# Weight-block differences of the FFNs' first pairs: formed by accumulating transfers in the place of VectorE's subtractions

## The chip, the cores and the metric

The kernel runs on one core of a Trainium2 chip. The metric is the device time of one execution in microseconds (us), as the median of several runs. Engines are named as the profile names them: PE is TensorE, DVE VectorE, ACT ScalarE, POOL GpSimd, SP SyncE.

## The reference

One layer of an encoder, 1024 tokens, model width 1024, FFN width 2816, float32. Only the two FFNs matter here:

```python
def swiglu(x, w_gate, w_up, w_down):
    return (jax.nn.silu(x @ w_gate) * (x @ w_up)) @ w_down
...
h = h + 0.5 * swiglu(rms_norm(h, ffn1_norm[i]), ffn1_w_gate[i], ffn1_w_up[i], ffn1_w_down[i])
...
h = h + (g_attn * y_attn + g_ssm * y_ssm) @ w_out[i]
h = h + 0.5 * swiglu(rms_norm(h, ffn2_norm[i]), ffn2_w_gate[i], ffn2_w_up[i], ffn2_w_down[i])
```

Between them lie attention and a state-space mixer, whose parameters are prepared by small operations while the first FFN runs.

## The kernel before

**Split products.** Every float32 operand is split into a high and a low part, so that one product is three matmuls of 128 x 512: high by high (L180), high by low (L181), low by high (L182). `split` (L148) makes the parts of a tile: ACT casts the high part (L149), DVE subtracts it from the source to get the low one (L150). Parts of weights are named wh and wl, parts of the x side xh and xl.

**Seven products.** The FFN matmuls are done in blocks of two by two by a scheme with seven products in the place of eight. The width 2816 is cut into 22 blocks of 128, which form 11 pairs, p = 0 to 10. Pair 0 is done plainly. In each other pair there are 14 items ("A", p, i, g): product i = 0 to 6, g = gate or up. An item is 12 matmuls into PSUM banks named gx, gy, gz, ux, uy, uz. In pair 1 the x operands (s1 to s4 and plain blocks) are still being made by DVE (L494 to L503) and split; later pairs use them again. After the A items come the B items of the down projection.

**Weight operands.** For each p and g there are four raw blocks b11, b12, b21, b22, tiles of `hbuf`, and `b_operand` (L421) makes the operand of product i out of them, in place, and splits it:

```python
if i in (2, 3, 6):
    V.tensor_tensor(b11, (b12, b22, None, None, b21)[i - 2], b11, ALU.subtract)
elif i == 5:
    V.tensor_tensor(b12, b22, b12, ALU.subtract)
hi, lo = tw("wh", [P, HT]), tw("wl", [P, HT])
mark["ins"] = split(hi, lo, (b21, b11, b11, b11, b22, b12, b11)[i]).ins
```

So the operands are: b21 for i = 0, b11 for 1, b12 - b11 for 2, b22 less that for 3, b22 for 4, b22 - b12 for 5, and b21 less the block that product 3 left in b11 for 6. Below, "(1,5,gate)" is the item p = 1, i = 5, g = gate. The down projection calls `b_operand` too, for its own tiles (wblk).

**Loads.** `load_two` (L460, its DMA at L465) brings b11 and b12, or b21 and b22, of one p and g with one transfer of 512 KB on SP's queue, as soon as the tiles of pair p - 2 are free. In pairs 1 and 2 one k is loaded ahead of the other.

**Order.** `run` (L697) prepares operands `la` items ahead: 4 in the first FFN, 8 in the second. PE's order is the program's throughout. DVE and ACT follow the program's order up to item (2,0,gate) of the first FFN; after that a scheduler orders them when the program is built. POOL and SP are ordered by it all through. Each engine carries out its instructions in order, so one that waits holds back all behind it. Evacuations (`evac_a`): for i = 0, 2, 3 ACT copies the bank (L576); for others DVE adds it to an earlier one (L580), then ACT applies silu for the gate (L584) or DVE multiplies gate and up (L586); `combine` (L531 to L539) makes four sums of hidden blocks.

**Beside it.** In the first FFN a generator prepares the mixer: POOL copies columns of `pw` into g_pe and g_pg (L867, L870), then multiplies them into gm, tv, em, tg (L922 to L924); PE transposes the results (L947, L958).

Of the kernel before, what the change touches and what calls it, by code (L numbers as in the profile page):

```python
# [11 lines left out]
AF = mybir.ActivationFunctionType  # L12
ALU = mybir.AluOpType
# [5 lines left out]
HT = 512  # L19
# [19 lines left out]
def encoder_block(ctx, tc, I, out):  # L39
    nc = tc.nc  # L40
    V, A, G, T = nc.vector, nc.scalar, nc.gpsimd, nc.tensor
# [26 lines left out]
    def at(kind, shape, dt, name):  # L68
        pool, tag, bufs = cur[kind]
        return pool.tile(list(shape), dt, tag=tag, bufs=bufs, name=name)  # L70
# [4 lines left out]
    def tw(name, shape=(P, 1024), dt=F32R):  # L75
        return at("w", shape, dt, name)
# [60 lines left out]
    def force():  # L137
        side["wait"] = 0
        tick()
# [8 lines left out]
    def split(hi, lo, src, eng=V):  # L148
        A.copy(hi, src)  # L149
        return eng.tensor_tensor(lo, src, hi.bitcast(F32), ALU.subtract)  # L150
# [267 lines left out]
                    self.put(name, self.h[j0 + k][1])  # L418
                    yield 1

    def b_operand(blk, i):  # L421

        b11, b12, b21, b22 = blk
        if i in (2, 3, 6):
            V.tensor_tensor(b11, (b12, b22, None, None, b21)[i - 2], b11, ALU.subtract)  # L425
        elif i == 5:
            V.tensor_tensor(b12, b22, b12, ALU.subtract)
        hi, lo = tw("wh", [P, HT]), tw("wl", [P, HT])
        mark["ins"] = split(hi, lo, (b21, b11, b11, b11, b22, b12, b11)[i]).ins
        return hi, lo  # L430

    NP2 = NF // 2
    C4 = ("11", "12", "22", "21")

    class Ffn:
# [175 lines left out]
        def prep(self, item):  # L611
            if item[0] == "C":
                _, c, g = item
                if c in ("11", "12") and not self.seven.plain:
                    for n in ((0, 2) if c == "11" else (1, 3)):
                        if ("C", g, n) in self.made:
                            continue
                        hi, lo = self.two[n, g]
                        mark["ins"] = split(hi, lo, self.blocks[0][g][n]).ins
                        self.made["C", g, n] = hi, lo  # L620
                return
            if item[0] == "A":
                _, p, i, g = item
                while self.stage < (1 if i < 2 else 2, 3)[p > 1]:
                    force()
                self.made[item] = b_operand(self.blocks[p][g], i)
                return
            _, i, j = item
            raw = self.kept.pop((i, j))
            hi, lo = at("tmp", [P, HT], F32R, "ah"), at("tmp", [P, HT], F32R, "al")  # L630
            split(hi, lo, raw)
            self.made[item] = (hi, lo), b_operand(self.blocks["d", j], i)
# [799 lines left out]
    for hp in range(4):  # L1432
# [3 lines left out]
        n = 2 if hp < 3 else 6  # L1436
# [294 lines left out]
```

## Time and profile before

| | us |
|---|---|
| median of 3 runs | 2145.44 (2139.88 to 2147.64) |
| the profiled execution | 2143.34 |
| its span in the trace | 2141.6 |
| PE busy | 2099.0 (98%) |
| DVE busy | 1423.1 (66%) |
| ACT busy | 986.9 (46%) |
| POOL busy | 395.0 (18%) |

The span runs from the first to the last record of the trace. Rows of a timeline carry the start of an instruction, its duration, and in brackets the engine's idle time before it with what ended the wait. Windows give the busy time of each engine in a stretch of the span and the clock granted to PE there, as a share of full speed. Mean durations overlap by the engines' pipelines: DVE's 128 x 512 subtractions show 0.68 us each, and follow each other every 0.60 to 0.61.

### The profile page before, as it was taken

The page shows a single profiled execution, that of the slowest core. Times are in us where ns is not written, and L with a number is a line of the kernel's source. Part 1 is how long each engine was busy: PE and PEld are TensorE (multiplying, and loading weights), DVE is VectorE, ACT ScalarE, POOL GpSimd, SP SyncE. Part 2 cuts the span into 40 slices and gives each one's busy share as a digit, 9 for nine tenths or more (in the row PEclk, how much of TensorE's full clock was granted, in tenths as well). Part 3 has the DMA queues.
Part 4 walks back from the last instruction along what each step waited for, and adds up shares of the span by engine and source line. Part 5 has one row for each costly group of instructions (what it writes and reads, how often), then busy time and mean ns, then how long its engine had stood idle before and what let it go on. Part 6 is the DMA issues. An engine that isn't in the chain of part 4 may idle for free.

```text
span 2141.6 us, 28452 instructions
## 1 busy us (share of the span) xinstructions
PE 2099.0 (98%) x9708; PEld 1718.3 (80%) x9708; DVE 1423.1 (66%) x2462; ACT 986.9 (46%) x1831; POOL 395.0 (18%) x680
## 2 busy tenths in 40 slices
PE   8999999999999999999999999999999999999997
PEld 3688888878888888888887788788888888888886
DVE  7886776666967334767744666896566565785845
ACT  6433333334445334666874432553333334445643
POOL 0047555540000008888000000000000000000000
PEclk9999999999999999999999999999999999999998
DMA  3524343466533452223576732242423338533302
GB/s 131 160 84 158 121 139 119 143 213 227 183 115 117 141 177 81 70 75 100 147 212 213 238 100 64 95 155 85 134 83 110 107 99 288 169 106 92 118 21 79
DMA packets 201105, 282.06 MB, mean 132 GB/s; under 512 B 42624, under 2 KB 85760, under 8 KB 200960
## 3 DMA queue, kind: packets, MB, share of 16 engines
q1 hardware_dynamic: 186112, 259.27, 38.1%
q10 hardware_dynamic: 14848, 20.98, 2.8%
q8 instruction: 76, 1.25, 0.3%
q14 instruction: 69, 0.57, 0.1%
HBM read 197.86 MB, written 82.31 MB: 131 GB/s over the span
## 4 chain that ended last, share of the span: by engine, by line
PE 87%; DVE 4%; DMA 4%; ACT 3%; issue 1%; SPq 1%; DVEq 0%; ACTq 0%
PE dx L180 4%; PE dx L181 4%; PE dx L182 4%; PE gx L180 3%; PE gx L182 3%; PE gx L181 3%; PE ux L180 3%; PE ux L182 3%; PE ux L181 3%; PE dy L180 2%; PE dy L182 2%; PE dy L181 2%; PE uy L180 2%; PE gy L180 2%; PE gy L182 2%; PE uy L182 2%
## 5 line engine op out<-in xcount | busy, mean ns | idle before, releaser
L149 ACT CAST wh<-hbuf 128x512 fp32r<-128x512 f32 x280 | 173.0, 622 | 396.0 <-PE gx L181 87.3
L150 DVE TENSOR_TENSOR wl<-hbuf,wh 128x512 fp32r<-128x512 f32 x280 | 208.9, 748 | 129.7 <-ACT wh L149 129.4
L149 ACT CAST wh<-wblk 128x512 fp32r<-128x512 f32 x162 | 100.4, 622 | 162.7 <-PE dx L181 67.5
L150 DVE TENSOR_TENSOR al<-araw,ah 128x512 fp32r<-128x512 f32 x154 | 106.2, 693 | 57.3 <-PE dx L181 19.7
L150 DVE TENSOR_TENSOR wl<-wblk,wh 128x512 fp32r<-128x512 f32 x162 | 112.1, 694 | 43.1 <-ACT wh L149 39.0
L180 PE MATMUL dx<-ah,wh 128*128 128x512 f32 x352 | 138.1, 392 | 0.5 <-DVE hbuf L693 0.5
L182 PE MATMUL dx<-ah,wl 128*128 128x512 f32 x352 | 137.0, 389 | 0.0
L181 PE MATMUL dx<-al,wh 128*128 128x512 f32 x352 | 137.0, 389 | 0.0
L1095 POOL TENSOR_TENSOR sc<-X,rho 128x128 f32<-128x128 f32 x128 | 72.4, 566 | 341.8 <-ACT X L1078 331.8
L180 PE MATMUL gx<-xh,wh 128*128 128x512 f32 x320 | 125.8, 393 | 5.7 <-DVE c L580 5.7
L182 PE MATMUL gx<-xh,wl 128*128 128x512 f32 x320 | 125.3, 391 | 0.0
L181 PE MATMUL gx<-xl,wh 128*128 128x512 f32 x320 | 125.0, 391 | 0.0
L180 PE MATMUL ux<-xh,wh 128*128 128x512 f32 x320 | 124.8, 390 | 0.0
L182 PE MATMUL ux<-xh,wl 128*128 128x512 f32 x320 | 124.5, 389 | 0.0
L181 PE MATMUL ux<-xl,wh 128*128 128x512 f32 x320 | 124.5, 389 | 0.0
L149 ACT CAST ah<-araw 128x512 fp32r<-128x512 f32 x154 | 94.9, 619 | 51.8 <-PE dx L181 12.6
L180 PE MATMUL gt<-xh,wh 128*128 128x512 f32 x256 | 103.2, 403 | 0.0
L182 PE MATMUL gt<-xh,wl 128*128 128x512 f32 x256 | 100.2, 392 | 0.0
L181 PE MATMUL gt<-xl,wh 128*128 128x512 f32 x256 | 100.1, 391 | 0.0
L425 DVE TENSOR_TENSOR hbuf<-hbuf 128x512 f32<-128x512 f32 x120 | 89.1, 743 | 2.5 <-DMA hbuf<-in_wu 0.5
L180 PEld LDWEIGHTS dx<-ah,wh 128*128 128x128 f32 x352 | 66.1, 188 | 15.9 <-DVE hbuf L693 1.7
L181 PEld LDWEIGHTS dx<-al,wh 128*128 128x128 f32 x352 | 66.1, 188 | 13.9 <-issue 0.5
(375 smaller groups left out, 5761.4 us busy)
## 6 DMA issues: line engine op xcount, KB each, us to landing
araw<-a_d SPq DMA_DIRECT2D x154, 256.0 KB
a_d<-c SPq DMA_DIRECT2D x148, 256.0 KB
wblk<-in_wd SPq DMA_DIRECT2D x88, 256.0 KB
hbuf<-in_wg SPq DMA_DIRECT2D x40, 512.0 KB
hbuf<-in_wu SPq DMA_DIRECT2D x40, 512.0 KB
wst<-in_win SPq DMA_DIRECT2D x26, 512.0 KB
hbuf<-in_xT SPq DMA_DIRECT2D x32, 256.0 KB
h_d<-hbuf ACTq DMA_DIRECT2D x32, 256.0 KB
```

Source lines behind the costliest of these rows:

```text
L149: A.copy(hi, src)
L150: return eng.tensor_tensor(lo, src, hi.bitcast(F32), ALU.subtract)
L180: T.matmul(o, lhsT=wh, rhs=xh, start=first, stop=False, skip_group_check=more)
L181: T.matmul(o, lhsT=wh, rhs=xl, start=False, stop=False, skip_group_check=more)
L182: T.matmul(o, lhsT=wl, rhs=xh, start=False, stop=last, skip_group_check=more)
L425: V.tensor_tensor(b11, (b12, b22, None, None, b21)[i - 2], b11, ALU.subtract)
L1095: G.tensor_tensor(sc, both, rho4, ALU.mult)
```

## The change

In pairs 1 to 3 of the first FFN and pairs 1 and 2 of the second, `b_operand` gets `src`, the four blocks of the weights in HBM. It subtracts nothing then. After the split of product 1, 2 or 3 it calls `taken_from`: ACT negates a raw block in place, and POOL issues a transfer of 256 KB that adds a block of the weights from HBM to it. After product 1, b11 becomes b12 - b11; after product 2, b11 becomes b22 less that and b12 becomes b22 - b12; after product 3, b11 becomes the operand of product 6. Each block's subtraction is thereby replaced by one negation and one transfer, four for each p and g, and the transfer is issued one or more products ahead of the operand's use. Lines below move by 10 or 13.

```diff
--- before.py
+++ after.py
@@ -418,15 +418,25 @@
                     self.put(name, self.h[j0 + k][1])
                     yield 1
 
-    def b_operand(blk, i):
+    def taken_from(blk, i, src):
+
+        A.activation(blk[i], blk[i], AF.Copy, scale=-1.0)
+        G.dma_start(blk[i], src, accum_op=ALU.add)
+
+    def b_operand(blk, i, src=None):
+
 
         b11, b12, b21, b22 = blk
-        if i in (2, 3, 6):
+        if src is None and i in (2, 3, 6):
             V.tensor_tensor(b11, (b12, b22, None, None, b21)[i - 2], b11, ALU.subtract)
-        elif i == 5:
+        elif src is None and i == 5:
             V.tensor_tensor(b12, b22, b12, ALU.subtract)
         hi, lo = tw("wh", [P, HT]), tw("wl", [P, HT])
         mark["ins"] = split(hi, lo, (b21, b11, b11, b11, b22, b12, b11)[i]).ins
+        if src is not None and i in (1, 2, 3):
+            taken_from(blk, 0, src[(1, 3, 2)[i - 1]])
+            if i == 2:
+                taken_from(blk, 1, src[3])
         return hi, lo
 
     NP2 = NF // 2
@@ -623,7 +633,10 @@
                 _, p, i, g = item
                 while self.stage < (1 if i < 2 else 2, 3)[p > 1]:
                     force()
-                self.made[item] = b_operand(self.blocks[p][g], i)
+                src = None
+                if p < (4 if self.seven.plain else 3):
+                    src = [self.w[g][p + (n % 2) * NP2][:, (n // 2) * HT:(n // 2 + 1) * HT] for n in range(4)]
+                self.made[item] = b_operand(self.blocks[p][g], i, src)
                 return
             _, i, j = item
             raw = self.kept.pop((i, j))
```

**Where the orders differ.** First DVE in pair 1 of the first FFN, at the operands of (1,2,gate) and (1,2,up). The names c_434 and c_438 are the same tile; s_315 and the like are x operands. Before:

```order
L558 TENSOR_TENSOR c_434<-g_397,rs_113 128x512 [waits PE_49]
L425 TENSOR_TENSOR hbuf<-hbuf 128x512 [waits DMAHW1_49]
L150 TENSOR_TENSOR wl<-hbuf,wh 128x512 [waits Activation_49]
L500 TENSOR_TENSOR s_315<-s_315,hbuf 128x512
L500 TENSOR_TENSOR s_318<-s_318,hbuf 128x512
L500 TENSOR_TENSOR s_321<-s_321,hbuf 128x512
L150 TENSOR_TENSOR xl<-s_315,xh 128x512 [waits Activation_49]
L500 TENSOR_TENSOR s_331<-s_331,hbuf 128x512
L150 TENSOR_TENSOR xl<-s_318,xh 128x512 [waits Activation_49]
L425 TENSOR_TENSOR hbuf<-hbuf 128x512 [waits DMAHW2_49]
```

and with the change:

```order
L568 TENSOR_TENSOR c_438<-g_397,rs_113 128x512 [waits PE_49]
L150 TENSOR_TENSOR wl<-hbuf,wh 128x512 [waits DMASW0_49,Activation_49]
L510 TENSOR_TENSOR s_315<-s_315,hbuf 128x512
L510 TENSOR_TENSOR s_318<-s_318,hbuf 128x512
L510 TENSOR_TENSOR s_321<-s_321,hbuf 128x512
L150 TENSOR_TENSOR xl<-s_315,xh 128x512 [waits Activation_49]
L510 TENSOR_TENSOR s_331<-s_331,hbuf 128x512
L150 TENSOR_TENSOR xl<-s_318,xh 128x512 [waits Activation_49]
```

L425 is gone, and wl waits for a transfer of POOL's queue (DMASW) beside ACT's cast.

Second ACT, from the cast of (1,4,up) to the first cast of pair 2, with the change (L586 and L594 are L576 and L584 of before). The two L423 wait for a transfer of SP's queue (DMAHW1, DMAHW2) and are the negations of b12 of pair 3; the first stands ahead of the cast of (1,6,gate), the second behind that of (2,0,gate).

```order
L149 CAST wh<-hbuf 128x512
L586 COPY c_610<-uy 128x512 [waits PE_49]
L149 CAST wh<-hbuf 128x512 [waits DMASW3_49]
L586 COPY c_641<-gx 128x512 [waits PE_49]
L149 CAST wh<-hbuf 128x512 [waits DMASW5_49]
L586 COPY c_659<-ux 128x512 [waits PE_49]
L423 ACTIVATE hbuf<-hbuf 128x512 [waits DMAHW1_49,DVE_49]
L149 CAST wh<-hbuf 128x512 [waits DMASW7_49]
L594 ACTIVATE c_641<-c_641 128x512 [waits DVE_49]
L149 CAST wh<-hbuf 128x512 [waits DMASW0_49]
L149 CAST wh<-hbuf 128x512 [waits DMAHW6_49,PE_49]
L423 ACTIVATE hbuf<-hbuf 128x512 [waits DMAHW2_49,Activation_49]
```

The casts of (1,5,gate) to (1,6,up), which waited for DVE before, now wait for transfers of POOL's queue (DMASW), and the negations of b12 for loads.

Third POOL, at the end of the generator's copies, in pair 3 of the first FFN. Before:

```order
L870 COPY g_pg<-pw 128x16
L867 COPY g_pe<-pw 128x16
L922 TENSOR_TENSOR gm<-g_pg,bb 128x512 [waits Pool_49]
L923 TENSOR_TENSOR tv<-g_pg,bb 128x512 [waits DMAHW1_49,Pool_49]
L922 TENSOR_TENSOR em<-g_pe,bc 128x576 [waits DVE_49,Pool_49]
L923 TENSOR_TENSOR tg<-g_pe,bc 128x576
L924 TENSOR_TENSOR gm<-gm,tv 128x512 [waits Pool_49]
L924 TENSOR_TENSOR em<-em,tg 128x576 [waits Pool_49]
```

and with the change, where L880 and L883 are the copies and L935 to L937 the products:

```order
L883 COPY g_pg<-pw 128x16
L880 COPY g_pe<-pw 128x16
L424 DMA hbuf<-in_wg 128x512 [waits DMAHW3_49,DMASW2_49,Activation_49]
L424 DMA hbuf<-in_wu 128x512 [waits DMAHW4_49,DMASW3_49,Activation_49]
L935 TENSOR_TENSOR gm<-g_pg,bb 128x512 [waits Pool_49]
L936 TENSOR_TENSOR tv<-g_pg,bb 128x512 [waits DMAHW1_49,Pool_49]
L935 TENSOR_TENSOR em<-g_pe,bc 128x576 [waits DVE_49,Pool_49]
L936 TENSOR_TENSOR tg<-g_pe,bc 128x576
L937 TENSOR_TENSOR gm<-gm,tv 128x512 [waits Pool_49]
L424 DMA hbuf<-in_wg 128x512 [waits DMASW4_49,Activation_49]
L424 DMA hbuf<-in_wu 128x512 [waits DMASW5_49,Activation_49]
L937 TENSOR_TENSOR em<-em,tg 128x576 [waits Pool_49]
```

The transfers of pair 3's products 2 stand behind all copies, those of product 3 behind five of the generator's products.

## Rows read from the trace of the kernel before

**Rows 1.** The page: busy time by engine, and one group of the costliest ones.

```profile
PE 2099.0 (98%) x9708; PEld 1718.3 (80%) x9708; DVE 1423.1 (66%) x2462; ACT 986.9 (46%) x1831; POOL 395.0 (18%) x680
...
L149 ACT CAST wh<-hbuf 128x512 fp32r<-128x512 f32 x280 | 173.0, 622 | 396.0 <-PE gx L181 87.3
```

**Rows 2.** PE's waits: line, releaser, us in total, times, longest us.

```profile
PE gx L180 <- DVE c L580: 5.7, 2, 4.5
```

**Rows 3.** PE's timeline: start us, us, operation [idle time before it, releaser].

```profile
64.69 0.80 PE L180 MATMUL gz<-xh,wh 128*128 128x512 f32 x1
...
102.46 0.47 PE L180 MATMUL gx<-xh,wh 128*128 128x512 f32 x1 [4.53 <-DVE c L580]
...
103.42 0.63 PE L180 MATMUL gx<-xh,wh 128*128 128x512 f32 x1
...
106.89 0.39 PE L180 MATMUL ux<-xh,wh 128*128 128x512 f32 x1
...
158.62 0.39 PE L180 MATMUL gy<-xh,wh 128*128 128x512 f32 x1
...
164.06 0.39 PE L180 MATMUL gx<-xh,wh 128*128 128x512 f32 x1
```

**Rows 4.** Windows: stretch, length, busy us by engine, PEclk, DMA share, GB/s.

```profile
94.00:98.00 4.00, 3.94 (x18) 2.84 (x16) 2.83 (x5) 1.71 (x4) 0.97 (x3) 1.00 0.84 239
...
104.00:106.00 2.00, 2.00 (x7) 1.52 (x6) 1.97 (x4) 0.01 (x1) 0.00 (x0) 0.50 0.20 77
...
110.00:150.00 40.00, 40.00 (x178) 33.12 (x177) 36.74 (x125) 15.50 (x28) 15.45 (x57) 1.00 0.30 100
...
1400.00:1450.00 50.00, 50.00 (x222) 41.39 (x221) 44.73 (x74) 24.53 (x45) 0.00 (x0) 1.00 0.49 163
1450.00:1500.00 50.00, 50.00 (x223) 41.38 (x222) 32.72 (x52) 17.95 (x31) 0.00 (x0) 1.00 0.27 90
```

**Rows 5.** DVE's groups by line, 64.5 to 102 us: busy, mean ns | idle before.

```profile
L150 DVE TENSOR_TENSOR wl<-hbuf,wh 128x512 fp32r<-128x512 f32 x11 | 7.6, 690 | 5.7 <-ACT wh L149 5.7
L425 DVE TENSOR_TENSOR hbuf<-hbuf 128x512 f32<-128x512 f32 x6 | 4.1, 684 | 0.0
...
L427 DVE TENSOR_TENSOR hbuf<-hbuf 128x512 f32<-128x512 f32 x2 | 1.4, 682 | 0.0
```

**Rows 6.** DVE's timeline in pair 1 of the first FFN.

```profile
61.70 2.50 DVE L150 TENSOR_TENSOR wl<-hbuf,wh 128x512 fp32r<-128x512 f32 x4 [1.21 <-ACT wh L149]
...
67.41 0.69 DVE L150 TENSOR_TENSOR wl<-hbuf,wh 128x512 fp32r<-128x512 f32 x1 [0.69 <-ACT wh L149]
...
88.28 0.69 DVE L150 TENSOR_TENSOR wl<-hbuf,wh 128x512 fp32r<-128x512 f32 x1 [0.74 <-ACT wh L149]
...
101.63 0.68 DVE L580 TENSOR_TENSOR c<-gx,c 128x512 f32<-128x512 f32 x1
```

**Rows 7.** SP's timeline (loads issued), then ACT's (waits for loads).

```profile
1.19 0.41 SPq L981 DMA_DIRECT2D hbuf<-in_xT  x1
...
89.00 0.54 SPq L465 DMA_DIRECT2D hbuf<-in_wg  x1
...
1399.19 0.56 SPq L465 DMA_DIRECT2D hbuf<-in_wg  x1
...
3.85 1.28 ACT L345 ACT_TABLE_LOAD   x1 [3.85 <-DMA hbuf<-in_xT]
...
1403.14 0.62 ACT L149 CAST wh<-hbuf 128x512 fp32r<-128x512 f32 x1 [0.92 <-DMA hbuf<-in_wg]
```

**Rows 8.** POOL's timeline in pairs 2 and 3 of the first FFN.

```profile
147.61 0.21 POOL L870 COPY g_pg<-pw 128x16 f32<-128x16 f32 x1
...
152.32 0.67 POOL L870 COPY g_pg<-pw 128x16 f32<-128x16 f32 x1
...
154.57 1.05 POOL L922 TENSOR_TENSOR gm<-g_pg,bb 128x512 f32<-128x512 f32 x1
...
159.77 1.75 POOL L924 TENSOR_TENSOR gm<-gm,tv 128x512 f32<-128x512 f32 x1
```

## The prediction

> **What bounds the kernel now.** I read the busy shares first: PE is busy 2099.0 us, 98% of the span [rows 1]. So whatever DVE is relieved of pays only where PE waits for DVE. The second view, PE's waits, lists one wait in the stages that the change touches, gx at L180 behind DVE's L580: 5.7 us in two stalls, the longest 4.5 [rows 2]. PE's timeline places that one in pair 1 of the first FFN, before item (1,6,gate): PE is idle for 4.53 us up to 102.46 [rows 3]. The rest of the windows say that there is no second place: PE is busy 3.94 of the last 4 us before it, 40.00 of 40 from 110 to 150, and 50.00 of 50 in both windows of the second FFN's pairs 1 and 2 [rows 4].
>
> The stall costs more than its idle time. After it the granted clock stands at 0.50 (the 1.2 GHz level) from 104 to 106 [rows 4], and one matmul shows 0.63 us where it shows 0.39 before [rows 3]. The item that follows the gap runs from 102.46 to 106.89, 4.43 us; the 14 items of a pair at full clock follow each other at 2.72 us (the two from 158.62 to 164.06 take 5.44) [rows 3]. So the stall costs 4.53 + 1.71 = 6.2 us, and that is all that the change can win from PE: 0.29% of the run. A measurement of this kernel tells about 0.5%, 10.7 us, from no change.
>
> **Why DVE is late there.** Between 64.5 and 102 us DVE runs L425 six times and L427 twice, each 0.68 us long, and before eleven wl it stands idle 5.7 us in all, behind ACT's cast wh [rows 5]. The chain of one operand is visible in [rows 6]: subtract, wait for ACT's cast, wl. DVE's own order then puts L580 on gx behind all of it, at 101.63 [rows 6], and PE waits for its end.
>
> **The change, part by part.** *Removed:* 40 subtractions, 24 in pairs 1 to 3 of the first FFN and 16 in pairs 1 and 2 of the second. In pair 1 the eight free 8 x 0.60 us (DVE's pitch: 2.50 us for four, less 0.69 for the last, by three [rows 6]) plus most of the 5.7 us of waiting, some 10 us. In the other four stages PE never waited, so those 32 are worth nothing.
>
> *Added on ACT:* 40 negations. No row shows one; a cast of the same tile takes 622 ns on ACT [rows 1], and I take that. *Added on POOL and the DMA engines:* 40 accumulating transfers of 256 KB. The trace has none. Call D the time from the negation's end to the landed sum. From below: a plain 256 KB load, issued at 1.19, had landed by 3.85, 2.66 us [rows 7]. From above: a 512 KB load issued at 1399.19 releases ACT's cast at 1403.14, 3.95 us [rows 7]; two of these in series (the sum must read and write its destination too) and the longest POOL row of 1.75 us for the issue [rows 8] make 9.6. I take 4.5: the sum touches twice the bytes of a 256 KB load, as the 512 KB load does (3.95), and an issue costs 0.54 on SP [rows 7].
>
> POOL is not a neutral place to issue from. Its small copies take 0.21 us alone and 0.67 beside DVE's two-input operations [rows 8]; an issue slowed in that ratio would add about 1 us to D. The Trainium skill has a rule that speaks against this (SBUF — State Buffer, SBUF: two separate sides): descriptors of transfers issued from GpSimd are written by GpSimd and starve while VectorE runs an operation in a 2-port mode. It also says that a two-input operation contends only with GpSimd's reads; no run here shows an issue beside either. By the Trainium skill, DMA: Bandwidth & Descriptors (Anatomy of one DMA), the transfer itself would be 2.0 us plus bytes at 436 GB/s, an estimate of 2.6 us, and the sum would be that of the first rival below.
>
> **The walk with D = 4.5.** *Pair 1.* The third of the four wl that start at 61.70 ends near 63.6 [rows 6]; negation to 64.2; landed 68.7; cast and wl of (1,2,gate) end at 70.1, where the wl of before ended at 68.10. ACT now has two negations, 1.2 us, ahead of the two xh casts, so (1,3,gate) ends its wl near 78.2 and (1,3,up) near 81.3, 1.7 us later than before. PE wants them at 64.69 + 6 x 2.72 = 81.0 and 83.7, so nothing stalls; the x operand s4, delayed by the same 1.7, still arrives. From there on DVE gains: wl (1,5,gate), which ended at 88.97 [rows 6], loses a subtraction and a cast wait (1.34) and ends near 89.3; the rest of the way to L580 on gx loses three subtractions and three waits, 3.9 us, so gx could start near 98.1. But a new wait sits in ACT's queue: the negation of pair 3's b12 stands ahead of the cast of (1,6,gate), and it needs a load that SP issues only when wl (1,5,gate) has freed its buffers (89.00 before [rows 7]). At 3.95 to 5 us landing, ACT resumes at 93.3 to 94.3, and wl (1,6,gate) and gx slip by up to 1.5. PE, which wants gx at 97.9, then waits 1 to 2.5 us instead of 4.53, and gets a shorter dip of clock: loss 3 us in the place of 6.2. **Term: -3.2.**
>
> *Pair 2.* Operands are prepared four items beyond the one at work, up to 13.6 us ahead; two steps of D + 1.9 (cast, wl, negation) against a cadence of 5.44 lose 2 x 1.0 us of it. Term 0.
>
> *Pair 3.* Its sums for products 2 stand in POOL's queue behind the generator's copies, those for product 3 behind gm, tv, em, tg, gm as well. The copies ended before at 154.57 [rows 8], but many of them were slowed by DVE, which now stands still itself, blocked in its order at wl (3,2,gate) from about 145, but for four combine operations. At 0.21 us they end near 150; landed 154.5; wl 155.7. PE wants (3,2,gate) at 158.62 [rows 3]. The second sum needs that wl, its negation and POOL's five products (7.0 us, from 154.57 to the end of the fifth at 161.52 [rows 8]): issued near 158, landed 162.5, cast 163.1, and PE wants it at 164.06 [rows 3]. Cover of 0.9 us, thin; if the copies end 2 us later it is gone and a stall of 1 us and part of a dip follow. **Term: 0 to +3, taken as +0.7.** POOL's own products are late by 2 to 3 us and their transposes on PE still come after.
>
> *Second FFN.* Operands are made further ahead there, POOL has no other work, and PE is at 50.00 of 50: term 0 as long as D is under some 12 us. The extra reading there (16 x 256 KB, 4.2 MB) falls into 100 us that move 163 and 90 GB/s, against 239 GB/s in the four us with most DMA work around the stall [rows 4]; I count no delay for it.
>
> Sum: -3.2 + 0.7 = -2.5, on the profiled execution's 2143.34 us: 2140.8. That execution lies 2.1 below the median of 2145.44, so the forecast for a median is **2143**.
>
> **The rivals.** *1. The stall goes entirely, nothing comes for it* (D near 2.7, copies fast, pair 3's load not late): 2145.4 - 6.2 = 2139. For it: eight subtractions and their waits are worth twice the stall. Against: each sum is now a negation, an issue and a transfer, where 0.68 us stood. Chance 0.20.
>
> *2. The stall is only moved* (D of 5.5 to 7). Pair 1: products 2 and 3 run 2.5 to 4 us later, s4 and gx slip with them, and the loss is again about 6; pair 3's cover of 0.9 is overdrawn by up to 2 us plus a dip of up to 1.7. Then 0 to +5: 2145 to 2150. For it: POOL's slowed copies, and the thin cover. Chance 0.28.
>
> *3. Slower.* The mechanism is the serial chain of cast, wl, negation and landing from product 1 to 2 to 3. At D = 9 it is 10.9 us a step. Pair 1: first sum landed 73.2, second 84.1, cast 84.7 against 81.0 wanted, 3.7 us, and as much again at s4 and gx; with two dips of 1.7 near 10 us in the place of 6.2, +4. Pair 3: first sum landed 159, 1 us late; the second, negated near 162, landed 171, cast 171.6 against 165.1, 6.5 us, and 1.7 of clock: +9. Together +13: 2158. Each microsecond of D costs about 4 us here, so it is slower than 0.5% from D of about 8.5 on. For it: the upper bound of 9.6, and that nothing in the trace shows such a transfer. Chance 0.15.
>
> *4. The change does not do what it says:* the orders show the 40 subtractions gone and 40 transfers there, so this is at most a transfer that the program makes wait for more than it must; 0.02, and it would look like rival 2.
>
> **How the numbers follow.** The forecast has 0.35. All cases but rival 3 lie within 10.7 us of 2145.4; they hold 0.85. Of it 0.02 go to faster by more than that, which would need more than all of the stall and so something that I have not seen, and 0.01 to slower, for a rival 2 that costs twice as much: same 0.82, slower 0.16 with rival 3. The range takes in rivals 1 and 2 with 2 us below for the spread of the runs, and rival 3 up to D = 9: 2137 to 2159. The likeliest case says that a large edit moves the time by 0.1%.
>
> **What would show it.** Right: the subtractions of weight tiles at 90 and 30 in the place of L425's 120 and L427's 40; PE's wait gx behind the combine line down from 4.5 to between 1 and 2.5 us near 98; ACT standing behind a load of in_wg just before; no PE idle time in pair 2 or in the second FFN; POOL's copies at 145 to 150 mostly 0.21; and accumulating transfers of 4 to 5 us. Wrong: a wait of PE for a cast wh of products 2 or 3, in pair 1 near 75 to 84 or in pair 3 near 158 to 165, with a granted clock below 1.00 behind it; landings above 8 us would make the prediction fail as a whole.

## The result and the profile after

The changed kernel takes 2148.65 us (median of 13 runs) where the kernel before takes 2143.30 (median of 13): ratio 1.0032, 95% interval 1.0022 to 1.0041. The two medians lie 5.4 us apart; the ratio, which is estimated from all the runs, stands for about 7 us. So the kernel is slower, inside the range that was given, and on the other side of the forecast, which said 2.5 us faster.

PE's waits for DVE's adds in the changed stages (line, releaser, us in total, times, longest; before: [rows 2]):

```profile
PE gx L180 <- DVE c L590: 7.2, 3, 3.7
...
PE ux L180 <- DVE c L590: 2.7, 1, 2.7
```

The one stall of 4.53 us [rows 3] has become several. PE's timeline says where (start, duration, operation, idle time before it):

```profile
87.00 0.47 PE L180 MATMUL ux<-xh,wh 128*128 128x512 f32 x1 [2.71 <-DVE c L590]
...
103.45 0.47 PE L180 MATMUL gx<-xh,wh 128*128 128x512 f32 x1 [2.57 <-DVE c L590]
...
164.88 0.50 PE L182 MATMUL gx<-xh,wl 128*128 128x512 f32 x1 [0.59 <-DVE wl L150]
...
1455.29 0.80 PE L180 MATMUL gx<-xh,wh 128*128 128x512 f32 x1 [3.73 <-DVE c L590]
1455.88 0.63 PE L181 MATMUL gx<-xl,wh 128*128 128x512 f32 x1
```

There are two in pair 1 of the first FFN, 2.71 and 2.57 us, a trace of one in pair 3, and one of 3.73 us in the second FFN, where there was none. The windows (busy us of PE, PEld, DVE, ACT, POOL; then PEclk, DMA share, GB/s; before: [rows 4]) show the same, and what the clock did:

```profile
50.00:100.00 50.00, 47.29 (x177) 33.04 (x176) 37.22 (x65) 28.27 (x52) 12.13 (x20) 1.00 0.72 184
100.00:150.00 50.00, 47.43 (x209) 38.96 (x209) 38.02 (x130) 22.72 (x43) 21.85 (x77) 1.00 0.65 167
...
1400.00:1450.00 50.00, 50.00 (x222) 41.44 (x221) 33.40 (x55) 28.03 (x51) 10.49 (x12) 1.00 0.85 214
1450.00:1500.00 50.00, 46.27 (x192) 37.71 (x192) 29.54 (x46) 20.83 (x36) 3.49 (x4) 0.93 0.43 113
```

The two stalls of pair 1 are followed by no dip, PEclk is 1.00 in both windows; the stall of the second FFN is, with 0.63 us a matmul where 0.39 is usual and a clock of 0.93 over its window. PE carries out the same 9708 matmuls in the same order in both kernels, so their starts can be set against each other one by one. From the start of the span to 106 us the changed kernel gains 0.6 us, by 170 us it has lost 1.1 again, and from 1450 to 1462 it loses 6.8: 3.73 idle and most of the rest, some 3, to the clock. Together +7.3. (In between, this one execution of the kernel after gains 4.0 us in attention and the mixer, which the change leaves alone, mostly because two dips of the clock in the execution before, near 1141 and 1233, are missing in it. That is why its span of 2144.9 is only 3.3 us longer.)

What stands behind each stall is in DVE's and ACT's timelines. DVE:

```profile
81.95 0.69 DVE L150 TENSOR_TENSOR wl<-hbuf,wh 128x512 fp32r<-128x512 f32 x1 [3.14 <-ACT wh L149]
...
86.17 0.68 DVE L590 TENSOR_TENSOR c<-ux,c 128x512 f32<-128x512 f32 x1
...
96.55 0.18 DVE L769 TENSOR_SCALAR g_prm<-g_prm 128x32 f32<-128x32 f32 x1 [1.84 <-DMA g_prm<-in_ssm_p]
...
1419.61 0.69 DVE L150 TENSOR_TENSOR wl<-hbuf,wh 128x512 fp32r<-128x512 f32 x1 [5.33 <-ACT wh L149]
...
1451.44 0.69 DVE L150 TENSOR_TENSOR wl<-hbuf,wh 128x512 fp32r<-128x512 f32 x1 [4.91 <-ACT wh L149]
...
1454.55 0.68 DVE L590 TENSOR_TENSOR c<-gx,c 128x512 f32<-128x512 f32 x1
```

ACT:

```profile
63.59 0.63 ACT L423 ACTIVATE hbuf<-hbuf 128x512 f32<-128x512 f32 x1 [0.92 <-DVE wl L150]
...
68.70 0.62 ACT L149 CAST wh<-hbuf 128x512 fp32r<-128x512 f32 x1 [0.66 <-DMA hbuf<-in_wg]
...
96.40 0.63 ACT L423 ACTIVATE hbuf<-hbuf 128x512 f32<-128x512 f32 x1 [5.78 <-DMA hbuf<-in_wg]
...
1444.06 0.63 ACT L423 ACTIVATE hbuf<-hbuf 128x512 f32<-128x512 f32 x1 [0.35 <-DVE wl L150]
...
1450.79 0.62 ACT L149 CAST wh<-hbuf 128x512 fp32r<-128x512 f32 x1 [4.20 <-DMA hbuf<-in_wg]
```

L423 is the negation, L149 the cast, L150 the wl, and L590 the add that evacuates a bank. In the second FFN ACT's cast at 1450.79 waited 4.20 us for a landing; DVE's wl behind it waited 4.91; behind that wl, in DVE's queue, stood the adds L590, the last of which (1454.55) frees the bank that PE waits for. At the first stall of pair 1 it is the same: a wl that waited 3.14 us until 81.95, the x operands behind it, and then L590 on ux at 86.17, which PE waits for until 87.00.

The transfers themselves, from the page (its group of POOL's issues, and its list of issues with the median us from issue to landing):

```profile
L424 POOL DMA_DIRECT2D hbuf<-in_wg x20 | 18.1, 946 | 506.9 <-DVE wl L150 396.1
...
hbuf<-in_wg POOLq DMA_DIRECT2D x20, 256.0 KB, 5.0
hbuf<-in_wu POOLq DMA_DIRECT2D x20, 256.0 KB, 5.0
```

### The profile page after: what moved, and what is told of

The parts are those of the page before. It is cut to its first block, busy times and chain, and to the rows that moved or that the text cites. A ratio compares the mean times of both kernels' runs of the same rounds, so it can differ in the third digit from the quotient of the medians.

```text
span 2144.9 us, 28522 instructions
## 1 busy us (share of the span) xinstructions
PE 2097.3 (98%) x9708; PEld 1716.7 (80%) x9708; DVE 1405.9 (66%) x2422; ACT 1006.8 (47%) x1871; POOL 420.4 (20%) x720
## 4 chain that ended last, share of the span: by engine, by line
PE 77%; DVE 8%; DMA 7%; issue 3%; ACT 3%; POOL 1%; SPq 1%; ACTq 0%; DVEq 0%; POOLq 0%
PE dx L180 4%; PE dx L181 4%; PE dx L182 4%; PE ux L180 3%; PE gx L180 3%; PE gx L182 3%; PE ux L181 3%; PE ux L182 3%; PE gx L181 3%; PE dy L182 2%; PE dy L181 2%; PE dy L180 2%; DMA hbuf<-in_wu 2%; PE gt L180 2%; PE gt L181 2%
## 5 line engine op out<-in xcount | busy, mean ns | idle before, releaser
L149 ACT CAST wh<-hbuf 128x512 fp32r<-128x512 f32 x280 | 172.9, 621 | 378.9 <-PE gx L181 80.7
L150 DVE TENSOR_TENSOR wl<-hbuf,wh 128x512 fp32r<-128x512 f32 x280 | 210.2, 754 | 155.6 <-ACT wh L149 155.2
L149 ACT CAST wh<-wblk 128x512 fp32r<-128x512 f32 x162 | 100.4, 622 | 160.5 <-PE dx L181 66.8
L150 DVE TENSOR_TENSOR al<-araw,ah 128x512 fp32r<-128x512 f32 x154 | 106.0, 692 | 57.9 <-PE dx L181 21.2
L150 DVE TENSOR_TENSOR wl<-wblk,wh 128x512 fp32r<-128x512 f32 x162 | 112.1, 694 | 42.4 <-ACT wh L149 38.4
L149 ACT CAST ah<-araw 128x512 fp32r<-128x512 f32 x154 | 94.9, 619 | 53.8 <-DMA araw<-a_d 15.0
L424 POOL DMA_DIRECT2D hbuf<-in_wg x20 | 18.1, 946 | 506.9 <-DVE wl L150 396.1
L180 PEld LDWEIGHTS gx<-xh,wh 128*128 128x128 f32 x320 | 60.6, 189 | 22.0 <-DVE c L590 5.5
```

The lines of the kernel that those rows point to most:

```text
L180: T.matmul(o, lhsT=wh, rhs=xh, start=first, stop=False, skip_group_check=more)
L424: G.dma_start(blk[i], src, accum_op=ALU.add)
```

## The experiments

Ratios are to the kernel before, run beside it on the same chip; stalls are those of one profiled execution each.

**Which stage costs it: e1, e2.** The condition in `prep` is cut to the first FFN (e1), or to the second (e2).

```diff
-                if p < (4 if self.seven.plain else 3):
+                if p < (4 if self.seven.plain else 0):     e1
+                if p < (0 if self.seven.plain else 3):     e2
```

> The change in the first FFN alone (pairs 1 to 3), nothing of it in the second. Theory A (the loss comes from the second FFN, where DVE's L590 adds stand in its queue behind a wl that waits for a sum): pair 1 gives -0.7 us, pair 3 takes +1.0, so within 1 us of the kernel before, ratio 0.9995 to 1.0005, and no PE wait of over 1 us between 1400 and 1500. Rival B (the loss comes from the first FFN, and the stall of the second FFN was chance of one execution): +5 to +7 us, ratio 1.0025 to 1.0035.

Measured 1.0009 (0.9998 to 1.0020). PE has no stall between 1400 and 1500. Its first FFN is that of the changed kernel, yet its two stalls of pair 1 are 3.02 and 1.52 us, where that showed 2.71 and 2.57: from one execution to the next a stall differs by up to about 1 us.

> The change in the second FFN alone (pairs 1 and 2). Theory A: PE waits 3 to 4.5 us for DVE's L590 near 1455 and the clock falls behind it, +5 to +6.5 us, ratio 1.0023 to 1.0030; pair 1 of the first FFN keeps its stall of 4.5 us. Rival B: within 1 us of before.

Measured 1.0037 (1.0023 to 1.0051), with a stall of 3.57 us near 1459 and one of 1.13. So the loss is the second FFN's (theory A); the first is even, within the uncertainty.

**What the removal alone is worth: e3.** `taken_from` is not called, and nothing is subtracted.

> The 40 subtractions are left out and nothing stands in their place: no negation, no accumulating transfer, so the operands of products 2, 3, 5 and 6 of those pairs are raw blocks. It is the most that the removal alone could win. Theory A: the 4.5 us stall in pair 1 and the dip of the clock go, nothing else moves: -5 to -6.5 us, ratio 0.9970 to 0.9977. Rival C (DVE's relief is worth nothing, because something else is late right behind it, such as ACT's casts): -0 to -2 us.

Measured 0.9965 (0.9954 to 0.9976), about 7.5 us faster (5 to 10). PE has no idle time left in pair 1:

```profile
50.00:100.00 50.00, 50.00 (x190) 35.50 (x189) 41.75 (x73) 24.95 (x45) 3.23 (x10) 1.00 0.52 171
100.00:150.00 50.00, 50.00 (x223) 41.40 (x222) 39.84 (x125) 19.44 (x35) 20.62 (x72) 1.00 0.25 85
```

The bound of the prediction, 6.2 us, lies inside that interval, and ACT's casts don't limit it. The replacement eats all of that and about as much again.

**Pair 1 of the first FFN: e4, e5.** e4 has the change in pair 1 only (`p < 2`, none in the second FFN). e5 has of it only the sums for products 5 and 6, each issued long before its use, and DVE's subtractions for products 2 and 3:

```diff
-        if src is None and i in (2, 3, 6):
+        if i in (2, 3) or src is None and i == 6:
...
-        if src is not None and i in (1, 2, 3):
-            taken_from(blk, 0, src[(1, 3, 2)[i - 1]])
-            if i == 2:
-                taken_from(blk, 1, src[3])
+        if src is not None and i == 3:
+            taken_from(blk, 0, src[2])
+        if src is not None and i == 2:
+            taken_from(blk, 1, src[3])
```

> The change in pair 1 of the first FFN alone. In the changed kernel two stalls, 2.7 and 2.6 us, stand in pair 1; before each, ACT stood at the negation of a b12 of pair 2 or 3 that waited for its load. Theory D (ACT's queue is blocked by loads of later pairs): with the later pairs left as they were, both stalls go or shrink below 1 us, and the kernel is 4 to 6 us faster than before, ratio 0.9972 to 0.9981. Rival E (the serial chain of cast, wl, negation and landing within pair 1 is late by itself): the first stall stays at 2 to 3 us, and the kernel is 0 to 3 us faster.

Measured 1.0002 (0.9993 to 1.0010), and PE's timeline keeps both stalls:

```profile
86.93 0.47 PE L180 MATMUL ux<-xh,wh 128*128 128x512 f32 x1 [2.35 <-DVE c L590]
...
103.47 0.47 PE L180 MATMUL gx<-xh,wh 128*128 128x512 f32 x1 [2.66 <-DVE c L590]
```

Theory D falls: with ACT's queue free of later pairs' negations, the wait of 5.78 us at 96.40 in the rows above included, nothing changed. That wait cost nothing, because DVE was as late for a reason of its own: in the rows above L769 waits until 96.55, ACT's negation until 96.40.

> Pair 1 of the first FFN alone, and only the two sums with a long lead: b22 - b12 for product 5 (negated after product 2) and b21 less b11 for product 6 (negated after product 3). Products 2 and 3 keep DVE's subtractions, so no operand waits for a landing in a series. Theory E (in pair 1 the first stall of 2.4 to 2.7 us comes from the serial chain of cast, wl, negation and landing, products 1 to 3): that stall is gone, and the second one, before (1,6,gate), is below 2.7 us; 3 to 6 us faster than before, ratio 0.9972 to 0.9986. Rival G (the second stall is the wait for the generator's load of g_prm, which is unchanged whatever DVE saves): the stall before (1,6,gate) stays at 2 to 2.7 us, 2 to 4 us faster.

Measured 0.9982 (0.9972 to 0.9992), 4 us faster. The first stall is gone, the second is not:

```profile
99.84 0.47 PE L180 MATMUL gx<-xh,wh 128*128 128x512 f32 x1 [2.35 <-DVE c L590]
```

So the first stall is the serial chain's (theory E). In this execution the second one is followed by a dip, with a clock of 0.97 from 100 to 150. For it, DVE's timeline of e5 has another wait:

```profile
93.19 0.18 DVE L769 TENSOR_SCALAR g_prm<-g_prm 128x32 f32<-128x32 f32 x1 [1.88 <-DMA g_prm<-in_ssm_p]
```

L769 takes the first of the generator's parameters, whose load can begin only when L572 has read the buffer that it reuses. SP's timeline has that load before, then in the changed kernel:

```profile
90.36 0.34 SPq L775 DMA_DIRECT2D g_prm<-in_ssm_p  x1
```

```profile
91.98 0.34 SPq L788 DMA_DIRECT2D g_prm<-in_ssm_p  x1
```

Before, the same line (L756) began at 93.61 without a wait, 3.25 us after the issue, and one L427 stood ahead of it. In the changed kernel L769 waits 1.84 us until 96.55, 4.57 us after the issue; in e5 it is 4.61. Ahead of the load on SP's queue stand two loads of 512 KB, at 89.41 and 90.61 (before, the last two were at 86.36 and 89.00). That these two make it land later is likely, but no run shows it alone. In e5, where DVE is relieved and has no chain, it comes to this line 2.3 us earlier than before and meets a load that it never waited for; in the changed kernel it comes 1.1 us later than before, and the load is later still.

**Is it that load: e9, e10, e13 to e16.** In e9 (late two sums) and e10 (all four, pair 1) the parameters got a new buffer, so that their load waits for nobody:

```diff
-        prm = gconst("prm", [P, 3, NPD])
+        prm = const("prm", [P, 3, NPD])
```

> The late two sums in pair 1 of the first FFN, and the generator's parameters (g_prm) in a buffer of their own, so that their load waits for no earlier reader and DVE's L769 for no load. Theory G (the 2.35 us left before (1,6,gate) are DVE's wait of 1.88 us for g_prm and what ACT makes of it): the stall falls to 0.7 us or less; 1.5 to 2.5 us faster than the late two sums alone, ratio to the kernel before 0.9968 to 0.9978. Rival K (ACT's casts behind its silu set the end): the stall stays at 1.5 to 2.4 us, ratio 0.9978 to 0.9985.

> All four sums in pair 1 of the first FFN as in the change, with the same buffer for g_prm. The first stall of 2.4 us, that of the serial chain, stays within 0.5 us; the second, 2.7 us, goes if theory G holds: ratio to the kernel before 0.9982 to 0.9992, against 1.0002 without the buffer. If rival K holds, 0.9995 to 1.0005.

Measured 1.010 (1.0082 to 1.0117) and 1.010 (1.0085 to 1.0115): about 21 us slower, for a reason of its own (e16). The stall before (1,6,gate) was gone in both traces, but the times could tell nothing. e13, e14 and e15 load the parameters into a buffer that is there already and that the mixer uses later (colm); no other buffer moves.

> The kernel before, with the generator's parameters loaded early into a buffer that the mixer uses later (no buffer moves). DVE did not wait for that load there, so both theory G and rival K expect the stall of 4.5 us to stay: within 1 us of before, ratio 0.9995 to 1.0005.

> The late two sums in pair 1 of the first FFN, with that buffer. Theory G (DVE's wait for g_prm is what keeps 2.35 us of stall): the stall before (1,6,gate) falls to 0.7 us or less, ratio 0.9967 to 0.9978, near the 0.9965 of the subtractions left out. Rival K (ACT's casts behind its silu): 1.5 to 2.4 us stay, ratio 0.9978 to 0.9988.

> All four sums in pair 1 as in the change, with that buffer. Theory G with E: the first stall (2.4 us, serial chain) stays, the second goes: ratio 0.9980 to 0.9992, against 1.0002 without the buffer. Rival K: 0.9995 to 1.0007.

Measured: e13 1.0000 (0.9990 to 1.0010); e14 0.9968 (0.9956 to 0.9981); e15 0.9990 (0.9979 to 1.0002). PE's stalls in e14, then in e15:

```profile
85.02 0.47 PE L180 MATMUL ux<-xh,wh 128*128 128x512 f32 x1 [0.37 <-DVE c L590]
...
99.12 0.47 PE L180 MATMUL gx<-xh,wh 128*128 128x512 f32 x1 [0.21 <-DVE c L590]
```

```profile
87.67 0.47 PE L180 MATMUL ux<-xh,wh 128*128 128x512 f32 x1 [3.19 <-DVE c L590]
...
101.77 0.47 PE L180 MATMUL gx<-xh,wh 128*128 128x512 f32 x1 [0.21 <-DVE c L590]
```

Theory G holds for pair 1 alone: with the load out of the way the second stall falls from 2.35 us (e5) to 0.21 in e14 and from 2.66 (e4) to 0.21 in e15, where the chain's stall of 3.19 stays. It is the stalls that decide; the interval of e15 overlaps what rival K expected too. e13 keeps the stall of 4.53 us. Not tried was the whole changed kernel with that buffer: there ACT's negation for pair 3 still waits until 96.40, so clearing the load alone may win little. e14, the late two sums of pair 1 with that buffer, beats both kernels: 2137.34 us against 2143.99 of the kernel before beside it.

> The kernel before, with the parameters in a new buffer of 384 bytes per partition, which moves all buffers placed after it. If the move alone slows PE, a window of 50 us of the FFNs holds 217 matmul records in the place of 222 and the time is 20 to 25 us more, ratio 1.009 to 1.012; if not, it is that of e13.

Measured 1.011 (1.0091 to 1.0128). The 384 bytes alone do it, for e13 takes the parameters out of their old buffer as well. In the window below PE never waits, and does fewer matmuls in the same 50 us at the same granted clock (222 before):

```profile
1500.00:1550.00 50.00, 50.00 (x217) 40.55 (x216) 30.83 (x49) 17.61 (x30) 0.00 (x0) 1.00 0.27 90
```

**How the second FFN loses it: e6, e7, e8, e11.** The condition is `not self.seven.plain and p == 1` in e6, `p == 2` in e7.

> The second FFN's pair 1 alone. Theory H (pair 2's wl, which wait for landings, stand in DVE's queue ahead of pair 1's last adds): with pair 2 left as it was, no stall near 1455, within 1 us of before. Rival I (pair 1's own sums delay s4 and so the loads of pair 2's blocks, and that is what is late): the stall stays at 2 us or more, +3 to +6 us.

> The second FFN's pair 2 alone. Theory H: the stall near 1455 stays, 3 to 4 us, and with its clock dip +5 to +6 us. Rival I: the loads are on time, the stall is below 1 us, within 1.5 us of before.

Measured: e6 1.0024 (1.0014 to 1.0034), e7 1.0000 (0.9989 to 1.0011). That is against theory H and for rival I: pair 1's sums alone make a stall, pair 2's alone make none of over 0.4 us. In e6, ACT's timeline shows first the wait for a sum of pair 1, later that for a load of pair 2's blocks, and PE's the stall:

```profile
1424.15 0.62 ACT L149 CAST wh<-hbuf 128x512 fp32r<-128x512 f32 x1 [3.36 <-DMA hbuf<-in_wg]
...
1448.44 0.62 ACT L149 CAST wh<-hbuf 128x512 fp32r<-128x512 f32 x1 [5.56 <-DMA hbuf<-in_wu]
```

```profile
1449.60 0.80 PE L180 MATMUL gy<-xh,wh 128*128 128x512 f32 x1 [3.79 <-ACT c L586]
```

The loads in the changed kernel, from SP's timeline, are late too. The stage's first load is issued 3.4 us earlier than before [rows 7], those of pair 2 from 1434.10 to 1441.93; before they were at 1431.02 to 1438.84. Against the stage that is 6.5 us late. Before, then in the changed kernel:

```profile
1431.02 0.55 SPq L465 DMA_DIRECT2D hbuf<-in_wg  x1
...
1438.84 0.55 SPq L465 DMA_DIRECT2D hbuf<-in_wu  x1
```

```profile
1395.82 0.56 SPq L475 DMA_DIRECT2D hbuf<-in_wg  x1
...
1434.10 0.55 SPq L475 DMA_DIRECT2D hbuf<-in_wg  x1
...
1441.93 0.54 SPq L475 DMA_DIRECT2D hbuf<-in_wu  x1
```

The other runs of the second FFN follow the same measure, from the stage's first load to the first of pair 2: 31.8 us before, 30.8 in e11 and 32.2 in e7, which have no stall of over 0.4 us; 38.3 in the changed kernel, 39.3 in e2 and 39.5 in e6, which have one of 3.6 to 3.8 us. Between them lies e12 (below), with 36.0 and a stall of 1.16.

> The change in the second FFN alone, with the wl of products 2 and 3 of its pairs 1 and 2 computed by POOL, so that DVE never waits for a landing in these products. Theory H: the DVE wait of 4.9 us ahead of its adds is gone, and the stall of PE near 1455 with it or down to below 2 us, since ACT's silu of (1,4,gate), behind the same waiting cast in ACT's queue, is what is left: 0 to +3 us. Rival J (the operands themselves are late for PE): the stall stays at 3.5 us or grows by POOL's longer subtraction, +5 to +8 us.

e8's edit gives `split` the engine `G if src is not None and i in (2, 3) else V`. Measured 1.0025 (1.0015 to 1.0036), about 5 us, with stalls of 1.26 and 2.38 us. Neither side came out as a whole: the time is what rival J expected, the stalls are not. They are 3.6 us together, against 4.7 in e2; that difference is about as large as the one between two executions, so it is not shown that relieving DVE's queue shortens them. ACT's queue keeps the rest: before the second stall DVE waits 3.25 us for a silu that stands behind a cast which waited 2.60 us for a landing.

```profile
1453.07 0.50 PE L180 MATMUL uy<-xh,wh 128*128 128x512 f32 x1 [1.26 <-ACT c L586]
...
1463.92 0.50 PE L180 MATMUL gx<-xh,wh 128*128 128x512 f32 x1 [2.38 <-DVE c L590]
```

> The late two sums in the second FFN's pairs 1 and 2 alone. Theory L (there the loss comes from the first sums of pair 1: their landings hold up DVE in its order, so s4 and with it the loads of pair 2's blocks come late): with products 2 and 3 back on DVE, no DVE wait of over 2 us between 1415 and 1430 and no stall of PE; within 1 us of before, ratio 0.9995 to 1.0005. Rival M (the transfers' traffic or ACT's negations delay the loads): half of the loss or more stays, ratio 1.001 to 1.003.

Measured 1.0004 (0.9991 to 1.0017), and PE never idle:

```profile
1400.00:1450.00 50.00, 50.00 (x222) 41.39 (x222) 43.70 (x72) 29.90 (x53) 4.48 (x5) 1.00 0.64 185
1450.00:1500.00 50.00, 50.00 (x222) 41.40 (x221) 31.11 (x48) 20.01 (x34) 2.60 (x3) 1.00 0.39 106
```

Here the two late sums cost nothing that can be seen, so the loss is that of the two early ones. Traffic and negations are halved, not gone, so a small share of theirs stays possible.

**What a landing is made of: e12.** `accum_op=ALU.add` is dropped.

> The changed kernel, but its 40 transfers copy the weight block over the negated one in the place of adding to it, so the operands are plain blocks. It prices the adding: if it is what makes a landing late, the time from the negation's end to the cast of (1,2,gate), 4.5 us with the sum, falls by 1 us or more; if the issue from POOL is, it stays within 0.3 us and the stalls with it.

One run, 2142.27 us, so no interval; the kernel before ran from 2138.80 to 2149.19 beside it. The page of e12, in the lines shown above of the changed kernel:

```profile
L424 POOL DMA_DIRECT2D hbuf<-in_wg x20 | 11.1, 555 | 503.7 <-DVE wl L150 396.0
...
hbuf<-in_wg POOLq DMA_DIRECT2D x20, 256.0 KB, 3.4
hbuf<-in_wu POOLq DMA_DIRECT2D x20, 256.0 KB, 3.5
```

An issue takes POOL 555 ns in the place of 946, and the median landing comes 1.5 us sooner (3.4 and 3.5 in the place of 5.0). The interval that was expected to tell, from the negation's end to the cast of (1,2,gate), falls from 4.48 to 3.73 us, which lies between the two expectations; the cast no longer waits for the landing there, but for ACT's own silu. Of the three stalls one nearly goes, one falls to a third, and the one before (1,6,gate), which is not the chain's, stays:

```profile
85.07 0.47 PE L180 MATMUL ux<-xh,wh 128*128 128x512 f32 x1 [0.55 <-DVE c L590]
...
101.27 0.47 PE L180 MATMUL gx<-xh,wh 128*128 128x512 f32 x1 [2.33 <-DVE c L590]
...
1453.55 0.50 PE L180 MATMUL gx<-xh,wh 128*128 128x512 f32 x1 [1.16 <-DVE c L590]
```

## Why the prediction was wrong

**The bound and the place** were right: 4.53 us and the clock behind it, 6.2 us in all, and e3 measured 7.5, with 5 to 10 possible.

**D** was right where nothing crowds it. The first sum's negation (63.59 + 0.63) ended at 64.22 and ACT's cast began at 68.70, 4.5 us, as taken; that value had been chosen between 2.7 and 9.6, so some of it is luck. With several sums and loads in flight it was more: the median from issue to landing is 5.0, and in the second FFN the cast at 1450.79 came 6.1 us after its negation's end. By the figures of the Trainium skill (DMA: Bandwidth & Descriptors, Anatomy of one DMA) such a transfer would take an estimate of 2.6 us; the traces of this kernel, in which other transfers run beside it, do not agree, neither at 5.0 with the adding nor at 3.4 without, and the measurement decides.

**The term of pair 1 (-3.2; measured -0.6)** failed at its step "so nothing stalls". It compared each operand's arrival with the item that uses it, and those were in time. It did not ask what else stands behind the waiting wl in DVE's queue: the add that frees the bank ux, which PE wants at 84.3 and gets at 87.0. The signs of being wrong looked in the wrong place too: they named a wait of PE for a cast, and PE waited for the adds. The rest of the term had a wait of 1 to 2.5 us before (1,6,gate), and 2.57 was measured, by luck. It was put down to ACT's negation of pair 3's b12, which did wait, until 96.40; but e4 has the same stall without it. DVE's wait for the parameters' load, for which it had never waited before, ended at 96.55 and is enough by itself (e4 with e15, e5 with e14).

**The term of pair 3 (+0.7; measured +1.1)** came out near, with a wait of 0.59 us for a wl at (3,3,gate), but its path was another. POOL's copies ended at 148.2, sooner than forecast, and its five products at 155.34, before the second sums were wanted; what was late was DVE. One of its four operations in `combine`, usually 0.68 us long, lasted past the end of those five products, of which the first began at 149.33:

```profile
148.79 7.11 DVE L545 TENSOR_TENSOR c<-c,c 128x512 f32<-128x512 f32 x1
```

So the wl of (3,2,gate), cast at 152.15, began only at 157.03 (forecast: to end at 155.7), and the second sums were issued at 158.74, behind ACT's negations. The walk had 158 for that, by luck.

**The term of the second FFN (0; measured +6.8)** is the step that turned the sign. It read "operands are made further ahead there ... term 0 as long as D is under some 12 us". Look-ahead covers a late operand. It does not cover what stands behind it on an engine that works in order: adds and copies that free PE's banks stand behind a wl that was placed ahead. (That a larger look-ahead makes this worse is likely, but no run varies it.) And the first two sums of pair 1 are not ahead at all: they hold DVE for 5.33 us at 1419.61, so s4 comes late, so the loads of pair 2's blocks, which overwrite what s4 reads, come 6.5 us late, and their casts hold ACT and DVE 30 us further on (e6, e7, e11). In the changed kernel pair 2's own sums come on top: the cast that waits at 1450.79 waits for one of them.

**The rivals.** Rival 3 had the mechanism of the serial chain and its price, about 4 us per microsecond of D, but looked for it in the first FFN and from 8.5 us on; here it decides at about 5 us, in the second. e12, with landings 1.5 us sooner, took 6 us less in its one run than the changed kernel's median, most of the loss.

## What to carry to other kernels

Before replacing a short operation by a long one with a wait, list what stands behind the wait in the order of every engine that takes part, above all what frees the banks and buffers of the bounding engine; the arrival of the operand itself is only half of the test. A transfer of 5 us in the place of a 0.6 us subtraction pays where its result is wanted 10 to 17 us later (products 5 and 6 in e14: 0.9968 with the load cleared), and costs where it stands in a chain (products 2 and 3). And an engine that is relieved can run into a load that it did not wait for before (e5): look for the next one in its order.

## What the runs showed of the hardware that was not expected

Adding is not free in a transfer issued from POOL: 946 ns to issue against 555, 5.0 us to land against 3.4 to 3.5, for the same 256 KB (means and medians of the 40 transfers in one execution each of the changed kernel and of e12).

A new buffer of 384 bytes per partition slowed PE's gate and up products in both FFNs by about 2% (from 1500 to 1550, 217 matmul records for 222; from 150 to 200, 227 for 231) at a granted clock of 1.00, 1.1% of the run (e16; e9 and e10 have it too). The matmuls of the down projection, 389 to 392 ns, are as before. Which buffer's place does it was not tried.

An operation of DVE in `combine` beside POOL's five products took 7.11 us in the place of 0.68 (the changed kernel at 148.79), and not by chance: 7.12 us in e1, and 6.25 for the one before it in e12. In the kernel before, which ran these products from 154.57 on, no operation of DVE beside them took over 1.9 us.

The length of a stall alone does not tell whether the granted clock falls to 0.50 behind it. It did behind the stalls of over 3.5 us (3.57 in e2, 3.73, 3.79 in e6, and those near 4.5), but also behind 2.33 (e12), 2.35 (e5) and 2.38 (e8); it did not behind 2.35 and 2.66 (e4), 2.57 and 2.71 (the changed kernel) and 3.19 (e15).
